# The end of a two-layer block's MLP: folds on another engine, the last eighth of the down projection in token order, and a parked residual in other buffers

## The chip, the cores and the metric

The kernel runs on one core of one Trainium2 chip. The metric is device time in microseconds (us); the number for a kernel is the median of several runs. Before the change it is 1811.55 us (three runs, 1811.48 to 1811.81).

## The reference, cut to what matters

Two layers act on a residual stream h of 512 tokens by 1024 features, in float32. Each layer has a mixer (attention and retention), then an MLP, then a gated per-layer embedding (PLE). The change lies between the MLP and the PLE gate:

```python
u = rms_norm(h, norm_mlp_pre[i])
ff = jnp.square(jax.nn.relu(u @ w_mlp_up[i])) @ w_mlp_down[i]      # 1024 -> 4096 -> 1024
h = h + rms_norm(ff, norm_mlp_post[i])
gate = jax.nn.sigmoid(rms_norm(h) @ w_ple_gate[i])                   # 1024 -> 1024
h = h + gate * rms_norm(p[i] @ w_ple_proj[i], norm_ple[i])
```

The norm of the MLP's output needs a sum over all 1024 features of a token, and so does the norm that feeds the gate. So the gate's product for a token can begin only after its whole row of the down projection is there.

## The kernel before, in words

**Precision.** Every matrix product is made of three: each operand is split into a rounded high part and a low part (the rest), and high x high, high x low and low x high are added in PSUM (the list `HL`). So each 128-row piece of a contraction takes three matmuls of 512 columns. For a weight tile of 128 x 1024 the high part is an ACT copy (L273) and the low part a DVE subtraction (L297). `chunk(key)` (L285) returns a split weight tile and, on the way, issues the fetches (`load`, L246, from SP) and the splits (`prefetch`, L266) of the items up to three ahead. The split tiles share a ring of five buffers (`wp`, L202), so a tile's split waits until the tile five items earlier has been read for the last time.

**Order of the work.** The order of TensorE's (PE) instructions is that of the program. The other engines' instructions are ordered by the framework's scheduler before the run; `soon` (L371) gives what it wraps a priority that is 300 places higher. `step` (L321) counts groups of matmuls; after a given number of them (`AGE_DN` = 6 for the down projection) it lets the oldest entry of `pending` issue its PE work. `settle` (L385) issues the entries of given token tiles at once. In `pre_norm` (L389) the second half of a norm, the four plus four PE transposes of a token tile with their evacuations on ACT (high part, L412) and DVE (low part, L413), is such an entry. Each group of four transposes needs one of the two PSUM banks named `tp`.

**The MLP.** The 4096 hidden features come in 32 groups of 128 (`up_job`). Seven eighths of the down projection (`UNITS` = 7) are done by a seven-product block scheme: each eighth has seven products `P1` to `P7` of combinations of hidden blocks with combinations of weight blocks (`product`, L839), and each product is added into an SBUF sum of 128 x 1024 (`prod`, L806, evacuated by DVE at L856). After the last unit the seven sums are combined by seven additions, the folds (`FOLD`, L807; issued at L907 on DVE): four behind `P6`, and one each behind `P3`, `P4` and `P2`. What is left in `P2`, `P3`, `P4`, `P5` is the output of seven eighths, for four token tiles of 128 and two halves of 512 features.

**The last eighth.** Its four hidden groups (`ff`, 28 to 31) are split into high and low parts directly: ACT takes the ReLU (L884) and the rounded square (L887), DVE the exact square (L888) and the low part (L889). The weights are four tiles: two per half of the output features. `row_job` (L328) runs the first half for the four token tiles together, weight tile by weight tile (four PSUM banks `acc`), and then the second half token tile by token tile. Each (token tile, half) has 12 matmuls in two steps of six. `evac_dn` (L919) adds or subtracts the sum in SBUF (DVE, L923), takes the sum of squares (ACT, L347), and multiplies by the norm's gain (L925: POOL for the first half, DVE for the second). After the second half it makes the row's factor (POOL, L355 and L357), updates the residual (DVE, L916), and starts the next norm (`pre_norm`: ACT L347, POOL L355 and L357, DVE L399).

**The parked residual.** Before the MLP, h is written to DRAM (`hm`). At L908 it is fetched back into four 128 x 1024 buffers of the group `A` (eight buffers, also used by the products' operands and the `ff` tiles). The group `X` has two buffers; it holds the sums of weight blocks that POOL makes for the block scheme (L258, L261) and, in the next layer, the two rope tables (`cs_tile`, L655).

**The gate.** `row_job` at L954 runs the PLE gate, first half of its features for token tiles 0 and 1, then 2 and 3. Each pair begins with `settle`.

Of the kernel before, what the change touches and what calls it, by code (L numbers as in the profile page):

```python
# [12 lines left out]
ALU = mybir.AluOpType  # L13
# [4 lines left out]
P = 128  # L18
S = 512
D = 1024  # L20
NL = 2
NT = S // P
# [19 lines left out]
ALL, PAIRS, ONES = ((0, 1, 2, 3),), ((0, 1), (2, 3)), ((0,), (1,), (2,), (3,))  # L42
# [3 lines left out]
AGE_DN = 6  # L46
# [9 lines left out]
UNITS = 7  # L56


def _dn(e, hf, k):
    return 8 * (e // 2) + 4 * hf + 2 * (e % 2) + k  # L60
# [138 lines left out]
def block(ctx: ExitStack, tc: tile.TileContext, x, pT, w, dl, gains, cs, lc, rel, eye, out):  # L199
    nc = tc.nc  # L200
# [11 lines left out]
    def blk(tag, shape, dt=F32, name="blk"):  # L212
        return big.tile(shape, dt, name=name, tag=tag, bufs=NAMES[tag])

    def t2(name="t2"):
        return tmp.tile([P, S], F32, name=name, tag="t")
# [4 lines left out]
    def bank(tag):  # L221
        b = banks[tag].pop(0)
        banks[tag].append(b)
        return b
# [41 lines left out]
    def prefetch(to_raw, to_split):  # L266
        while loaded[1] < min(to_split, len(ITEMS)):
            m = loaded[1]
            key, src = ITEMS[m]
            load(max([n for n in src if n != "chain"]) + 1)  # L270
            r = raw[src[0]] if len(src) == 1 else total(key, src)
            t = wp.tile([P, 2, 1024], F32R, name="wt", tag="wt", bufs=5)
            nc.scalar.activation(t[:, 0, :], r, AF.Copy)  # L273
            n = src[-1]
            pool = len(src) == 1 and (PLAN[n][1] in POOL_LOW and n % POOL_MOD or PLAN[n][1:] in POOL_MORE)
            for sl in HALVES if pool else (slice(0, D),):
                low(nc.gpsimd if pool else nc.vector, t[:, 1, sl], r[:, sl], t[:, 0, sl])
            wt[m] = t
            loaded[1] += 1
            for n in src:  # L280
                if LAST.get(n) == m:
                    raw.pop(n, None)
        load(to_raw)

    def chunk(*key):  # L285
        m = ITEM[key]
        n = max(x for _, src in ITEMS[max(0, m - 3):m + 4] for x in src if x != "chain")
        prefetch(n + 3, m + 4)
        return wt[m]
# [26 lines left out]
    def row_mm(ps, ch, j, lhs, k, t, first, last):  # L316
        for n, (a, b) in enumerate(HL):
            nc.tensor.matmul(ps, lhsT=lhs(a, k, t), rhs=ch[:, b, j * S:(j + 1) * S],  # L318
                             start=first and n == 0, stop=last and n == 2)

    def step(age=None):  # L321
        clock[0] += 1
        age = AGE if age is None else age
        if pending and clock[0] - pending[0][0] >= age:
            soon(pending.pop(0)[1])()
        tick()

    def row_job(keys, lhs, evac, groups=ALL, age=None):  # L328
        n = len(keys)
        chs = {}  # L330
        for grp in groups:
            if lhs is u_lhs:
                settle(grp)
            pss = [bank(ROW_BANKS[n]) for n in range(len(grp))]
            for c in range(len(keys)):
                if grp is groups[0]:
                    chs[c] = chunk(*keys[c])
                for t, ps in zip(grp, pss):
                    for j in range(2):
                        row_mm(ps, chs[c], j, lhs, 2 * c + j, t, c == 0 and j == 0, c == n - 1 and j == 1)  # L340
                    if c == n - 1:
                        evac(t, ps)
                    step(age)
# [27 lines left out]
    def soon(f, offset=None):  # L371
        offset = PRIO if offset is None else offset

        def g(*a):
            if not offset:
                return f(*a)
            with tc.high_priority(offset=offset):
                return f(*a)
        return g
# [5 lines left out]
    def settle(ts):  # L385
        while any(t in unready for t in ts):
            soon(pending.pop(0)[1])()
# [59 lines left out]
    def tick():  # L447
        if side["gen"] is None:
            return
        side["owed"] += side["rate"]  # L450
        while side["owed"] >= 1.0:
            side["owed"] -= 1.0
            if soon(lambda: next(side["gen"], None), BG)() is None:
                side["gen"] = None
                return
# [179 lines left out]
    def one_layer(i, h):  # L635
# [102 lines left out]
        h = [blk("V", [P, D], name="h") for _ in range(NT)]  # L738
# [3 lines left out]
        for c in range(8):  # L742
            th = ths[c] if c in ths else b_gate(c)
            ps = bank("acc")
# [37 lines left out]
        for hf in range(2):  # L782
            hsl = slice(hf * S, (hf + 1) * S)
            ch = chunk(i, "pp", hf)
            for t in range(NT):
                ps = bank(PP_BANKS[4 * hf + t])
# [19 lines left out]
        prod = {x: blk("V", [P, 2, S], name=f"sum{x}") for x in PROD}  # L806
# [4 lines left out]
        def dn_bank():  # L811
            b = dn_banks.pop(0)
            dn_banks.append(b)
            return b
# [7 lines left out]
        def operands(f1, f2):  # L822
            a11, a21, a12, a22 = f1[:, :, :256], f1[:, :, 256:], f2[:, :, :256], f2[:, :, 256:]
            ops = {}
            x, y, z, v = (t2(n).rearrange("p (s n) -> p s n", s=2) for n in ("sx", "sy", "sz", "sv"))
            operand(ops, "P1", a11)
            nc.vector.tensor_tensor(x, a22, a21, op=ALU.subtract)
            operand(ops, "P5", x)
            nc.vector.tensor_tensor(z, a11, a21, op=ALU.subtract)
            operand(ops, "P7", z)  # L830
            nc.vector.scalar_tensor_tensor(y, x, -1.0, a11, op0=ALU.mult, op1=ALU.subtract)
            operand(ops, "P6", y)
            nc.vector.scalar_tensor_tensor(v, y, -1.0, a12, op0=ALU.mult, op1=ALU.subtract)
            operand(ops, "P3", v)
            operand(ops, "P4", a22)
            operand(ops, "P2", a12)
            return ops
# [21 lines left out]
        for j in range(2):  # L859
            settle(PAIRS[j])  # L860
            for c in range(EARLY):
                if not j:
                    early.append(bank(EARLY_BANKS[c]))
                t = chunk(i, "up", c)
# [8 lines left out]
        half_f = []  # L873

        def up_job(c):
            if c < EARLY:
                ps = early[c]
            else:
                ps = bank("s")
                t_job((i, "up", c), ps)  # L880
            if 2 <= c < 6:
                ple_norm(c - 2)
            r = t2("relu")
            nc.scalar.activation(r, ps, AF.Relu)  # L884
            if c >= 4 * UNITS:
                b = blk("A", [P, 2, S], F32R, name="ff")
                nc.scalar.activation(b[:, 0, :], r, AF.Square)  # L887
                nc.vector.tensor_tensor(r, r, r, op=ALU.mult)  # L888
                nc.vector.tensor_tensor(b[:, 1, :], r, b[:, 0, :].bitcast(F32), op=ALU.subtract)  # L889
                half_f.append(b)  # L890
                return
            if c % 2 == 0:
                half_f.append(blk("P", [P, 2, S], name="f"))
            nc.scalar.activation(half_f[-1][:, c % 2, :], r, AF.Square)
# [3 lines left out]
        for e in range(UNITS):  # L898
            ops = operands(*half_f)
            half_f = []  # L900
            for n, xs in enumerate((("P1", "P5"), ("P7", "P6"), ("P3", "P4"), ("P2",))):
                up_job(4 * e + 4 + n)
                for name in xs:
                    product(e, name, ops[name])
                    if e == UNITS - 1:
                        for to, of in FOLD.get(name, ()):
                            nc.vector.tensor_tensor(prod[to], prod[to], prod[of], op=ALU.add)  # L907
        for t in range(NT):  # L908
            h[t] = blk("A", [P, D], name="hr")
            nc.sync.dma_start(h[t], hm[t])  # L910

        acc = [[prod[x][:, t % 2, :] for x in (("P2", "P3"), ("P4", "P5"))[t // 2]] for t in range(NT)]
# [6 lines left out]
        def evac_dn(hf):  # L919
            @soon  # L920
            def f(t, ps):
                a = acc[t][hf]
                nc.vector.tensor_tensor(a, ps, a, op=ALU.subtract if hf else ALU.add)  # L923
                ssq[t][hf] = sumsq(a, t2("junk"), None if hf else 1e-6)
                (nc.vector if hf else nc.gpsimd).tensor_tensor(a, a, g_mpost[:, HALVES[hf]], op=ALU.mult)  # L925
                if hf:
                    pre_norm(h[t], t, None, upd_mlp(t, rstd_of(*ssq[t])))
            return f

        for hf in range(2):  # L930
            row_job([(i, "dn", _dn(UNITS, hf, k)) for k in range(2)],
                    lambda a, k, t: half_f[k][:, a, t * P:(t + 1) * P], evac_dn(hf), ONES if hf else ALL, AGE_DN)

        if not last:
            g_next = gain_row(5 * (i + 1))
# [19 lines left out]
        if last:  # L955
            t, f = NT - 1, evac_pg(1)
            for j in range(CUTS):
                cut = slice(j * S // CUTS, (j + 1) * S // CUTS)
                n = cut.stop - cut.start
                ps = bank("acc")  # L960
# [9 lines left out]
    h = [blk("V", [P, D], name="h") for _ in range(NT)]  # L970
# [25 lines left out]
    for i in range(NL):  # L996
        h = one_layer(i, h)
# [29 lines left out]
```

## Time and profile before

| what | value |
|---|---|
| median of 3 runs | 1811.55 us |
| the profiled execution, its own time | 1810.16 us |
| its span (first to last instruction) | 1808.4 us |
| PE busy | 1773.1 us, 98% of the span |
| VectorE (DVE) busy | 1215.8 us, 67% |
| ScalarE (ACT) busy | 822.1 us, 45% |
| GpSimd (POOL) busy | 496.1 us, 27% |
| mean granted clock of TensorE | 0.994 |

How to read it: times in rows are us from the start of the span, unless ns is said. A timeline row gives start, length, engine, line, operation, output<-inputs, shapes and how many instructions it merges; in brackets stands the idle time of the engine before it and what ended it. Matmuls are pipelined: in a merged row the length divided by the count is their spacing, while a single one is listed as about 389 ns long. Some matmul records are missing, so counts can be a little low.

### The profile page before, as it was taken

The numbers are of one execution on the slowest core, as the hardware profiler recorded it, in microseconds if no ns is written. First come the engines' busy times: TensorE is split into PE (matmuls) and PEld (weight loads), VectorE is DVE, ScalarE is ACT, GpSimd is POOL, SyncE is SP. The second block draws the span as 40 slices with busy tenths as digits, with TensorE's granted clock in tenths as the row PEclk, the third lists the DMA queues.
The fourth block names the chain that finished last, engine by engine and source line by source line (L and its number), as shares of the span: only waits on it lengthen the run. The fifth ranks groups of instructions, "written<-read, shape, count | busy, mean of one in ns | idle before, by whom it ended". The sixth has DMA issues, their size and how long they took to land.

```text
span 1808.4 us, 22117 instructions
## 1 busy us (share of the span) xinstructions
PE 1773.1 (98%) x8185; PEld 1466.0 (81%) x8185; DVE 1215.8 (67%) x1839; ACT 822.1 (45%) x1291; POOL 496.1 (27%) x370
## 2 busy tenths in 40 slices
PE   8999999999999999998999999999999999999989
PEld 6888788888888888887888887888888888888867
DVE  6676768743557787788556767677444677777873
ACT  4355454422456454544343555443234574544442
POOL 2312144301165222222023222442012642222130
PEclk9999999999999999999999999999999999999989
DMA  5554464432343222334246545554232422333231
GB/s 214 200 182 157 156 209 148 144 140 93 111 146 117 94 94 97 113 122 158 94 140 212 166 149 171 180 164 169 98 112 97 137 94 99 111 107 104 94 140 47
DMA packets 79165, 243.10 MB, mean 134 GB/s; under 512 B 10961, under 2 KB 19537, under 8 KB 79058
## 3 DMA queue, kind: packets, MB, share of 16 engines
q1 hardware_dynamic: 79058, 241.70, 39.9%
q8 instruction: 64, 1.05, 0.2%
q14 instruction: 43, 0.35, 0.1%
HBM read 208.10 MB, written 33.55 MB: 134 GB/s over the span
## 4 chain that ended last, share of the span: by engine, by line
PE 87%; DVE 5%; POOL 3%; ACT 2%; issue 1%; DMA 1%; SPq 0%; ACTq 0%; POOLq 0%
PE acc L308 27%; PE s L308 17%; PE acc L318 17%; PE acc L845 10%; PE tp L845 5%; PE tp L608 2%; POOL wt L297 2%; PE tp L540 2%; PE tp L503 2%; PE acc L867 1%; ACT wt L273 1%; PE tp L409 1%; PE s L521 1%; DVE wt L297 1%; PE s L522 1%
## 5 line engine op out<-in xcount | busy, mean ns | idle before, releaser
L308 PE MATMUL acc<-uT,wt 128*128 128x512 f32 x1920 | 472.9, 393 | 0.0
L308 PEld LDWEIGHTS acc<-uT,wt 128*128 128x128 f32 x1920 | 356.5, 188 | 71.5
L273 ACT ACTIVATE wt<-raw 128x1024 fp32r<-128x1024 f32 x278 | 293.4, 1056 | 225.6 <-PE acc L308 114.5
L297 DVE TENSOR_TENSOR wt<-raw,wt 128x1024 fp32r<-128x1024 f32 x211 | 291.6, 1389 | 131.5 <-ACT wt L273 130.6
L318 PE MATMUL acc<-wt,uT 128*128 128x512 f32 x1320 | 324.2, 399 | 4.0 <-DVE uT L413 1.7
L308 PE MATMUL s<-uT,wt 128*128 128x512 f32 x1392 | 324.7, 389 | 0.0
L308 PEld LDWEIGHTS s<-uT,wt 128*128 128x128 f32 x1392 | 261.3, 188 | 54.0
L297 POOL TENSOR_TENSOR wt<-raw,wt 128x512 fp32r<-128x512 f32 x134 | 184.9, 1401 | 409.8 <-ACT wt L273 370.6
L318 PEld LDWEIGHTS acc<-wt,uT 128*128 128x128 f32 x1320 | 248.1, 191 | 55.8 <-DVE uT L413 2.9
L845 PE MATMUL acc<-wt,op 128*128 128x512 f32 x792 | 188.0, 389 | 0.0
L845 PEld LDWEIGHTS acc<-wt,op 128*128 128x128 f32 x792 | 148.7, 188 | 30.8
L261 POOL TENSOR_TENSOR wsum<-raw 128x1024 f32<-128x1024 f32 x28 | 74.7, 2667 | 210.1 <-DMA raw<-in_w_dram 210.1
L258 POOL TENSOR_TENSOR wsum<-wsum,raw 128x1024 f32<-128x1024 f32 x28 | 71.1, 2539 | 167.6 <-DVE wt L297 167.6
L856 DVE TENSOR_TENSOR sumP<-acc,sumP 128x512 f32<-128x512 f32 x112 | 75.5, 686 | 61.6 <-PE acc L845 61.1
L884 ACT ACTIVATE relu<-s 128x512 f32<-128x512 f32 x60 | 35.5, 592 | 175.7 <-PE s L308 175.7
L297 DVE TENSOR_TENSOR wt<-wsum,wt 128x1024 fp32r<-128x1024 f32 x56 | 83.9, 1498 | 15.4 <-ACT wt L273 15.4
L845 PE MATMUL tp<-wt,op 128*128 128x512 f32 x384 | 92.3, 389 | 0.0
L308 PE MATMUL acc<-retT,wt 128*128 128x512 f32 x384 | 89.3, 389 | 0.0
L845 PEld LDWEIGHTS tp<-wt,op 128*128 128x128 f32 x384 | 72.1, 188 | 14.9
L308 PEld LDWEIGHTS acc<-retT,wt 128*128 128x128 f32 x384 | 72.1, 188 | 14.9
L300 ACT ACTIVATE rt<-rz 128x512 fp32r<-128x512 f32 x64 | 40.3, 632 | 90.0 <-DVE rz L590 89.5
L526 ACT ACTIVATE z<-z,nm 128x512 f32<-128x512 f32 x64 | 46.2, 722 | 56.6 <-DVE nm L525 56.3
(166 smaller groups left out, 2232.3 us busy)
## 6 DMA issues: line engine op xcount, KB each, us to landing
raw<-in_w_dram SPq DMA_DIRECT2D x292, 512.0 KB, 3.3
kk<-stk SPq DMA_DIRECT2D x128, 128.0 KB, 4.1
stq<-rr SPq DMA_DIRECT2D x16, 512.0 KB, 3.4
qs<-stq SPq DMA_DIRECT2D x128, 64.0 KB, 2.8
stk<-rr SPq DMA_DIRECT2D x16, 512.0 KB, 3.0
stv<-vr SPq DMA_DIRECT2D x16, 512.0 KB, 4.8
vh<-stv SPq DMA_DIRECT2D x16, 512.0 KB, 4.3
gain<-in_gains_dram SPq DMA_DIRECT2D x9, 512.0 KB, 3.8
```

The source lines that it names most:

```text
L258: nc.gpsimd.tensor_tensor(r, r, b, op=ALU.add)
L261: nc.gpsimd.tensor_tensor(r, raw[src[0]], raw[src[1]], op=ALU.add)
L273: nc.scalar.activation(t[:, 0, :], r, AF.Copy)
L297: eng.tensor_tensor(dst, src, hi.bitcast(F32), op=ALU.subtract)
L300: nc.scalar.activation(dst[:, 0], src, AF.Copy, scale=scale)
L308: nc.tensor.matmul(ps, lhsT=t[:, a, (off + k) * P:(off + k + 1) * P], rhs=r, start=k == 0 and n == 0, stop=k == kts - 1 and n == 2)
L318: nc.tensor.matmul(ps, lhsT=lhs(a, k, t), rhs=ch[:, b, j * S:(j + 1) * S], start=first and n == 0, stop=last and n == 2)
L503: nc.tensor.matmul(o, lhsT=v, rhs=pt[k][:, hl, :], start=k == 0 and hl == 0, stop=k == 3 and hl == 1)
L526: nc.scalar.activation(z, z, AF.Exp, bias=nm, scale=-1.0, accum_out=den)
L540: nc.tensor.transpose(ps[:, t * P:(t + 1) * P], zs[t][:, k * P:(k + 1) * P], ident)
L845: nc.tensor.matmul(ps, lhsT=op[:, a, k, j * P:(j + 1) * P], rhs=t[:, b, k * S:(k + 1) * S], start=k == 0 and n == 0, stop=k == 1 and n == 2)
L856: nc.vector.tensor_tensor(a, ps, a, op=ALU.add)
```

## The change

The seven folds are issued on POOL instead of DVE. The parked residual of token tiles 0 and 1 is fetched into group `X` and only that of tiles 2 and 3 into `A`. The last eighth calls `chunk` for all its four weight tiles first and then runs token tile by token tile: for each, both halves of the features, each from four pieces of the contraction, with PSUM banks taken from the six that the products use (`dn_bank`: the four `acc` and the two `tp`). `evac_dn` and the step count are as before.

```diff
--- before.py
+++ after.py
@@ -904,9 +904,9 @@
                     product(e, name, ops[name])
                     if e == UNITS - 1:
                         for to, of in FOLD.get(name, ()):
-                            nc.vector.tensor_tensor(prod[to], prod[to], prod[of], op=ALU.add)
+                            nc.gpsimd.tensor_tensor(prod[to], prod[to], prod[of], op=ALU.add)
         for t in range(NT):
-            h[t] = blk("A", [P, D], name="hr")
+            h[t] = blk("X" if t < 2 else "A", [P, D], name="hr")
             nc.sync.dma_start(h[t], hm[t])
 
         acc = [[prod[x][:, t % 2, :] for x in (("P2", "P3"), ("P4", "P5"))[t // 2]] for t in range(NT)]
@@ -927,9 +927,16 @@
                     pre_norm(h[t], t, None, upd_mlp(t, rstd_of(*ssq[t])))
             return f
 
-        for hf in range(2):
-            row_job([(i, "dn", _dn(UNITS, hf, k)) for k in range(2)],
-                    lambda a, k, t: half_f[k][:, a, t * P:(t + 1) * P], evac_dn(hf), ONES if hf else ALL, AGE_DN)
+        tail = [chunk(i, "dn", _dn(UNITS, hf, k)) for hf in range(2) for k in range(2)]
+        for t in range(NT):
+            for hf in range(2):
+                ps = dn_bank()
+                for k in range(4):
+                    row_mm(ps, tail[2 * hf + k // 2], k % 2, lambda a, k, t: half_f[k][:, a, t * P:(t + 1) * P], k, t, k == 0, k == 3)
+                    if k == 3:
+                        evac_dn(hf)(t, ps)
+                    if k % 2:
+                        step(AGE_DN)
 
         if not last:
             g_next = gain_row(5 * (i + 1))
```

## Rows read from the trace of the kernel before

**Rows 1.** The page's first part: busy time and share of each engine.

```profile
PE 1773.1 (98%) x8185; PEld 1466.0 (81%) x8185; DVE 1215.8 (67%) x1839; ACT 822.1 (45%) x1291; POOL 496.1 (27%) x370
```

**Rows 2.** Timeline of PE, layer 0, last eighth to the gate's first product.

```profile
828.93 20.56 PE L318 MATMUL acc<-wt,ff 128*128 128x512 f32 x90
849.69 1.09 PE L409 MATMUL tp<-ident,un 128*128 128x128 f32 x8 [0.20 <-DVE un L399]
850.54 1.64 PE L318 MATMUL acc<-wt,ff 128*128 128x512 f32 x6
858.43 1.11 PE L409 MATMUL tp<-ident,un 128*128 128x128 f32 x4 [6.25 <-DVE ss L349]
860.99 1.12 PE L409 MATMUL tp<-ident,un 128*128 128x128 f32 x4 [1.45 <-DVE uT L413]
861.76 8.92 PE L318 MATMUL acc<-wt,uT 128*128 128x512 f32 x30
```

**Rows 3.** Timeline of PE, layer 1, the same two waits.

```profile
1753.56 1.11 PE L409 MATMUL tp<-ident,un 128*128 128x128 f32 x4 [6.25 <-DVE ss L349]
1756.12 1.12 PE L409 MATMUL tp<-ident,un 128*128 128x128 f32 x4 [1.45 <-DVE uT L413]
```

**Rows 4.** Windows of PE: length, busy (x), granted clock, DMA share, GB/s.

```profile
852.18:855.44 3.26, 0.00 (x1) 1.00 0.02 4
855.44:865.69 10.25, 5.81 (x17) 0.50 0.30 103
...
1747.31:1749.74 2.43, 0.00 (x0) 1.00 0.01 3
1749.74:1759.98 10.24, 4.97 (x15) 0.50 0.15 52
```

**Rows 5.** Timeline, layer 0: evacuations of the first transposed tile, ACT then DVE.

```profile
853.52 0.57 ACT L412 ACTIVATE uT<-tp 128x512 fp32r<-128x512 f32 x1
...
857.69 0.68 DVE L413 TENSOR_TENSOR uT<-tp,uT 128x512 fp32r<-128x512 f32 x1
...
860.26 0.68 DVE L413 TENSOR_TENSOR uT<-tp,uT 128x512 fp32r<-128x512 f32 x1
```

**Rows 6.** The folds: busy per engine from 811.9, the line L907, DVE's timeline.

```profile
811.90:832.60 20.70, 20.70 (x93) 17.12 (x92) 20.13 (x24) 7.32 (x9) 0.00 (x0) 1.00 0.48 175
...
L907 DVE TENSOR_TENSOR sumP<-sumP,sumP x14: 1214/1217/1228, 811.9 to 1725.8; 128x1024 f32<-128x1024 f32 x14
...
810.75 1.22 DVE L297 TENSOR_TENSOR wt<-raw,wt 128x1024 fp32r<-128x1024 f32 x1
...
824.99 2.35 DVE L297 TENSOR_TENSOR wt<-raw,wt 128x1024 fp32r<-128x1024 f32 x2
...
831.85 0.68 DVE L889 TENSOR_TENSOR ff<-relu,ff 128x512 fp32r<-128x512 f32 x1
```

**Rows 7.** Timeline where POOL and DVE meet in layer 0: POOL, then DVE.

```profile
718.15 2.40 POOL L258 TENSOR_TENSOR wsum<-wsum,raw 128x1024 f32<-128x1024 f32 x1 [12.61 <-DVE wt L297]
...
718.00 0.68 DVE L856 TENSOR_TENSOR sumP<-tp,sumP 128x512 f32<-128x512 f32 x1
718.60 4.17 DVE L297 TENSOR_TENSOR wt<-raw,wt 128x1024 fp32r<-128x1024 f32 x2
```

**Rows 8.** Timeline, three POOL operations in a row beside DVE; last row: DVE undisturbed.

```profile
505.39 4.69 POOL L297 TENSOR_TENSOR wt<-raw,wt 128x512 fp32r<-128x512 f32 x3
...
505.45 3.48 DVE L402 SCALAR_TENSOR_TENSOR un<-h,rstd,gain 128x512 f32<-128x512 f32 x2 [2.94 <-POOL rstd L357]
...
896.65 1.41 DVE L402 SCALAR_TENSOR_TENSOR un<-hr,rstd,gain 128x512 f32<-128x512 f32 x2 [1.69 <-POOL rstd L357]
```

**Rows 9.** Residual fetches (SP), their first use (DVE), first use of the rope tables.

```profile
826.65 2.79 SPq L910 DMA_DIRECT2D hr<-hm  x4
...
846.05 1.41 DVE L916 SCALAR_TENSOR_TENSOR hr<-sumP,rstd,hr 128x512 f32<-128x512 f32 x2 [0.71 <-DMA raw<-in_w_dram]
...
L472 DVE TENSOR_TENSOR ra<-acc,cst x4: 680/687/692, 940.0 to 957.0; 128x512 f32<-128x512 f32 x4
```

## The prediction
> **What bounds the kernel now.** I read the page's shares first: PE is busy 98% of the span [rows 1], so only what moves PE's end counts, and PE's remaining idle time is where to look. PE's timeline at the end of layer 0's last eighth [rows 2] shows it. Its 96 matmuls begin at 828.93 and go at 0.228 us each (20.56 / 90), 1.37 us per step of six. The transposes of token tile 0 come 15 steps in and wait 0.20 us for their norm. The eighth ends at 850.54 + 1.64 = 852.18; then PE waits 6.25 us before the transposes of tile 1 and 1.45 us between their two groups: 7.9 us idle. Layer 1 repeats the two large waits to the hundredth [rows 3].
>
> There is a second price. The granted clock is 1.00 up to 3.26 us into this idle time (2.43 us in layer 1), then 0.50, the lower of the two levels, for 10.24 us [rows 4]. PE is busy 5.81 us of that in layer 0 and 4.97 us in layer 1, so half is lost: 2.9 and 2.5 us. So this place costs 10.8 us in layer 0 and 10.4 us in layer 1, **21.2 us** in all.
>
> Why the wait? The row's releaser is a small DVE operation, but that is only the semaphore's last count. The tile-1 transposes need a `tp` bank that still holds tile 0's. ACT reads the first group at 853.52; DVE reads it only at 857.69 and the second at 860.26 [rows 5], and PE's two groups start right behind. DVE is late because the second half of the eighth hands it a whole token tile every two steps (2.7 us): two residual updates (1.41 as a pair, [rows 9]) and, of the same kind as the 0.68 us operations of [rows 5], one subtraction, one gain, two evacuations of the transposes, and two norm scalings: over 4.5 us.
>
> **The change part by part.**
>
> Token order. Each tile now takes four steps (5.5 us) and both its halves end together, so DVE gets about 5 us of work per 5.5 us, and the norm of tile 0 starts after step 4, not step 10. Today's tile-0 norm takes 7.2 us from the end of step 10 (842.5) to 849.69 [rows 2]; its transposes are still issued six counts later, after step 9, 5 steps or 6.8 us behind the evacuation: 0.4 us of wait. Tile 1's come after step 13, inside the eighth. So the two waits go, if DVE keeps up: minus 21.2, plus 0.4 per layer, plus about 0.6 per layer for the gate's first products waiting for tile 1's evacuation (between 0, if DVE is free, and the 1.45 us of [rows 2]).
>
> Folds. A fold costs DVE 1.22 us [rows 6], 1.14 from start to start (824.99 has two in 2.35). The nearest POOL row, an addition of the same shape, is 2.40 us [rows 7]. By busy time alone DVE gains 7 x 1.14 = 8.0 us of the 20.13 it is busy in the 20.7 us after the first fold [rows 6]. But DVE and POOL exclude each other here: a pair of L297, 2.35 us when POOL is idle, takes 4.17 us when it starts 0.45 us into a 2.40 us POOL addition: it waited for that to end [rows 6, 7]. DVE operations that read one operand from PSUM do not wait: L856 keeps its 0.68 us across the POOL operation's start [rows 7]. With several POOL operations in a row the two take turns: L402 pairs go from 1.41 to 3.48 us [rows 8]. The Trainium skill ("SBUF — State Buffer", section "Who interferes with whom") calls it an exclusive lock held for a whole instruction, taken by GpSimd operations that read SBUF and DVE operations with two SBUF inputs; the trace agrees. That page does not say who is next; if POOL kept the pair through the four folds behind `P6`, 9.6 us by the 2.40 us row, DVE would be blocked all that time at once; the turns of [rows 8] speak against it.
>
> So from 811.9 (the first L297 after `P6` ends, [rows 6]) I add up the lock. POOL needs 7 x 2.40 = 16.8 us. Until the last `ff` low part DVE has five L297 (1.14) and four of L888 and L889 (0.60) with both operands in SBUF: 8.1 us. With turns and no gap: 811.9 + 24.9 = 836.8, plus two evacuations of `P2` at 0.6 which the seventh fold itself awaits: **838.0**. If the seventh fold comes behind that low part, it is 835.6. Before, it was done at 832.5 [rows 6].
>
> Now who waits? Before, the pieces k = 2 and 3 of the contraction came after four steps, at 834.4; in the new order k = 3 comes with matmul 10, at 828.93 + 9 x 0.228 = 831.0. So PE waits **4.6 to 7.0 us** there. The clock would fall about 2.8 us into that wait (between the 2.43 and 3.26 of [rows 4]), at 833.8, until 844.1; PE, resuming at 835.6 to 838.0, runs 8.5 to 6.1 us at half speed and loses 4.3 to 3.0. Wait and clock together: 8.9 to 10.0 us per layer, oddly insensitive to the length of the wait.
>
> Residual in `X`. Today's fetches land some 6 us after 826.65, and the first use is at 846.05 [rows 9]; the first use moves to about 838, still covered. Nothing gained; at most 1 us if a fetch blocks SP's queue of weight fetches, which runs two items or more ahead. The next layer's rope tables must now wait until tiles 0 and 1 are done in the gate, near 896.65 + 1.41 [rows 8]; they are first used at 940.0 [rows 9], so nothing. The folds pass no other POOL work: POOL is idle there (0.00, [rows 6]).
>
> Four `chunk` calls first, six banks. The ring has five buffers and four are held by the eighth to its last steps, so the second gate tile is split only after step 13 instead of after step 4. From there to its use are 3 steps, the transposes of tile 1 and 2 gate steps, 7.6 us; its split needs two operations of 1.2 us (ACT's estimated from DVE's L297). Nothing, up to 2 us per tile if DVE is behind. The `tp` banks, now shared: tile 1's last subtraction (0.68) ends before tile 0's transposes: 0 to 0.5 us.
>
> **The sum.** Per layer: removed 10.8 or 10.4, added 8.9 to 10.0 plus 0.4 plus 0.6. Net -0.9 to +0.2 in layer 0 and -0.5 to +0.6 in layer 1; both layers -1.4 to +0.8. The profiled execution took 1810.16 us (span 1808.4), 1.4 below the median; added to it, 1810.2 to 1812.4. I say **1811.0 us**: a stall changes places. With 2 us more or less per layer for DVE's order, 1806.5 to 1815.
>
> **The rivals.**
>
> 1. Faster: the low part of `ff` 31 comes early in DVE's order, ahead of the last weights' L297, and only one or two folds delay it. For it: the 8 us that DVE is relieved of. Against: the lock sum. Without a lock it would be done at 831.4 (832.5 less a fold): wait 0.4; with two L297 behind it, 835.6 - 2.3 = 833.3: wait 2.3, short enough to keep the clock. With the 1.0 of the later waits and up to 1.5 for a late weight tile, the loss is 1.4 to 4.8 per layer in place of 10.6: 1811.55 - 2 x (5.8 to 9.2) = 1793 to 1800, likeliest 1797. Chance 0.25.
>
> 2. Slower: the weight ring. The stall stays as forecast, and behind it the gate's second to fourth weight tiles, freed one step apart at the eighth's end, queue on DVE behind the norms of tiles 2 and 3. Each L297 (1.14) has an in-order queue with some 5 us of norm work before it; it decides once the first is over 5 us late (7.6 less 2.4). Then PE waits 2 to 4 us per layer: 1815 to 1819. For it: DVE is the late engine there today [rows 5]. Against: token order spreads its work. Chance 0.19.
>
> 3. The change does not do what it says, as something else holds tile 1's transposes: time unchanged, inside the forecast's range; chance 0.01, the forecast 0.55.
>
> **How the numbers follow.** About 0.2% (3.6 us) is what a measurement of this kernel can tell from no change. Below 1807.9: rival 1 with 0.25 and the forecast's lower edge, 0.09. Above 1815.2: rival 2 with 0.18 and the forecast's upper edge, 0.07. The rest, 0.41, is no change. The range reaches into both rivals, 1796 to 1816.5, leaving out about 0.08 at either end.
>
> **What would show it.** Right: no idle time before L409 behind the eighth; a PE wait of 4 to 8 us at the tenth matmul of the eighth, released by DVE's L889; L297 and L889 beside the folds at 2 to 3.5 us; folds 2.4 to 3.6 us each; a window of clock 0.50 some 3 us into that wait. Wrong: L889 done before 833 and no half clock, or the 6.25 us wait still there.

## The result, and the profile after

The changed kernel takes 1822.62 us (median of 4 runs, 1821.28 to 1825.62); the kernel before took 1811.68 us (median of 4). The ratio is 1.0063, with a 95% interval of 1.0045 to 1.008: it is **slower** by 11 us. The forecast of 1811.0 us and its range, 1796 to 1816.5, missed it; its sign was that of the second rival.

The profiled execution took 1823.24 us (span 1821.5), 13.1 us of span more than before. This is PE's timeline of the changed kernel at the same place in layer 0, and the rows of layer 1 where it waits; it answers to [rows 2, 3].

```profile
829.58 2.65 PE L318 MATMUL acc<-wt,ff 128*128 128x512 f32 x11
838.54 5.15 PE L318 MATMUL acc<-wt,ff 128*128 128x512 f32 x13 [6.30 <-DVE ff L889]
...
851.27 0.66 PE L409 MATMUL tp<-ident,un 128*128 128x128 f32 x4 [0.78 <-DVE un L399]
852.33 0.66 PE L409 MATMUL tp<-ident,un 128*128 128x128 f32 x4 [0.40 <-DVE sumP L923]
...
860.20 0.66 PE L409 MATMUL tp<-ident,un 128*128 128x128 f32 x4 [1.28 <-DVE ss L349]
860.61 4.37 PE L318 MATMUL acc<-wt,ff 128*128 128x512 f32 x18
865.82 1.62 PE L318 MATMUL acc<-wt,uT 128*128 128x512 f32 x6 [0.84 <-DVE sumP L923]
870.02 4.56 PE L318 MATMUL acc<-wt,uT 128*128 128x512 f32 x12 [2.58 <-DVE sumP L923]
...
880.75 1.03 PE L409 MATMUL tp<-ident,un 128*128 128x128 f32 x8
...
1739.80 5.08 PE L318 MATMUL acc<-wt,ff 128*128 128x512 f32 x13 [6.30 <-DVE ff L889]
...
1771.20 4.55 PE L318 MATMUL acc<-wt,uT 128*128 128x512 f32 x12 [2.58 <-DVE sumP L923]
```

The old waits of 6.25 and 1.45 us are gone. In their place stand a wait of 6.30 us for the low part of the last hidden group (L889), three smaller ones at the transposes (2.46 us together), and two at the gate's first products for L923, the subtraction of the eighth's last token tile (0.84 and 2.58 us).

To compare versions I use one stretch, from the eighth's first matmul to the transposes of tile 3. In the changed kernel it is 880.75 - 829.58 = 51.17 us in layer 0 and 51.09 in layer 1. These are its last rows in the kernel before, layer 0 and 1:

```profile
874.15 1.03 PE L409 MATMUL tp<-ident,un 128*128 128x128 f32 x8
...
1768.86 1.03 PE L409 MATMUL tp<-ident,un 128*128 128x128 f32 x8
```

There it is 874.15 - 828.93 = 45.22 and 1768.86 - 1724.06 = 44.80 us. So the two stretches hold 5.95 + 6.29 = 12.2 of the 13.1 us; the rest is spread over the execution (0.65 us of it are there when the first stretch begins).

The windows of PE in the changed kernel (length, busy, granted clock, DMA share, GB/s) show that the clock falls twice per layer:

```profile
832.24:835.83 3.59, 0.00 (x0) 1.00 0.84 302
835.83:842.66 6.83, 4.12 (x10) 0.50 0.58 225
867.44:869.97 2.53, 0.00 (x0) 1.00 0.00 0
869.97:873.38 3.41, 3.36 (x8) 0.50 0.68 199
```

It falls 3.59 us into the wait for L889, for 6.83 us, and at the end of the 2.58 us wait, for 3.41 us. Half of the busy time in these is lost: 2.06 and 1.68 us.

Why L889 is late stands in DVE's timeline of the changed kernel, and then POOL's:

```profile
819.89 2.29 DVE L888 TENSOR_TENSOR relu<-relu 128x512 f32<-128x512 f32 x1
...
822.71 2.29 DVE L889 TENSOR_TENSOR ff<-relu,ff 128x512 fp32r<-128x512 f32 x1
824.91 0.68 DVE L856 TENSOR_TENSOR sumP<-tp,sumP 128x512 f32<-128x512 f32 x1
825.52 6.16 DVE L297 TENSOR_TENSOR wt<-raw,wt 128x1024 fp32r<-128x1024 f32 x2
...
833.93 0.68 DVE L888 TENSOR_TENSOR relu<-relu 128x512 f32<-128x512 f32 x1
834.53 3.35 DVE L297 TENSOR_TENSOR wt<-raw,wt 128x1024 fp32r<-128x1024 f32 x1
837.81 0.68 DVE L889 TENSOR_TENSOR ff<-relu,ff 128x512 fp32r<-128x512 f32 x1
...
811.57 10.06 POOL L907 TENSOR_TENSOR sumP<-sumP,sumP 128x1024 f32<-128x1024 f32 x3 [8.10 <-DVE sumP L856]
824.40 6.20 POOL L907 TENSOR_TENSOR sumP<-sumP,sumP 128x1024 f32<-128x1024 f32 x2
834.09 2.72 POOL L907 TENSOR_TENSOR sumP<-sumP,sumP 128x1024 f32<-128x1024 f32 x1 [3.49 <-DVE sumP L856]
```

A DVE operation with both operands in SBUF that meets a fold waits for it: 2.29 us for one of 0.68, 6.16 for a pair of 2.35 [rows 6]. The folds wait too: three take 10.06 us, not 7.2. Evacuations from PSUM (L856) keep their 0.68. The last fold begins at 834.09, between L888 and L889, and holds the L297 that stands between these; L889 ends at 838.49.

And this is DVE at the norms of tiles 0 and 1 and at the start of the gate, changed kernel, and then POOL:

```profile
849.72 1.89 DVE L399 TENSOR_SCALAR un<-hr,rstd 128x512 f32<-128x512 f32 x2 [1.03 <-POOL rstd L357]
...
857.58 1.97 DVE L399 TENSOR_SCALAR un<-hr,rstd 128x512 f32<-128x512 f32 x2 [0.43 <-POOL rstd L357]
...
866.19 0.87 DVE L399 TENSOR_SCALAR un<-hr,rstd 128x512 f32<-128x512 f32 x2
866.98 0.15 DVE L349 TENSOR_SCALAR ss<-ss 128x1 f32<-128x1 f32 x1
867.04 2.23 DVE L297 TENSOR_TENSOR wt<-raw,wt 128x1024 fp32r<-128x1024 f32 x1
869.20 0.68 DVE L923 TENSOR_TENSOR sumP<-acc,sumP 128x512 f32<-128x512 f32 x1
...
849.66 1.28 POOL L925 TENSOR_TENSOR sumP<-sumP,gain 128x512 f32<-128x512 f32 x1
...
857.98 1.28 POOL L925 TENSOR_TENSOR sumP<-sumP,gain 128x512 f32<-128x512 f32 x1 [0.44 <-ACT junk L347]
...
866.81 1.39 POOL L925 TENSOR_TENSOR sumP<-sumP,gain 128x512 f32<-128x512 f32 x1 [0.74 <-ACT junk L347]
```

The subtraction for tile 3 stands behind the norm of tile 2 and a low part of the gate's weights in DVE's order. Until it has run, the bank is not free, and the gate's second product has been given that bank.

The same rows show that POOL holds DVE up at a second place, where no fold is left. The gain of the first half (L925) is on POOL, as it was before, but in token order that of the next tile falls beside a norm. The pair of L399 at the gate takes 0.87 us; those of tiles 0 and 1, each beside an L925, take 1.89 and 1.97, although L399 reads only one tensor from SBUF. The L297 ahead of the last subtraction takes 2.23 us instead of 1.22, beside a third L925. So about 1.0 us each of the waits of 1.28 and 2.58 us, and all of the 0.78, is this (an estimate from these lengths). In the kernel before none of the 16 L399 takes over 0.49 us. No run here moves this gain to DVE.

### The profile page after: what moved, and what is told of

Read it like the earlier page. It is cut to its first block, busy times and chain, and to the rows that moved or that the text cites. A ratio compares the mean times of both kernels' runs of the same rounds, so it can differ in the third digit from the quotient of the medians.

```text
span 1821.5 us, 22108 instructions
## 1 busy us (share of the span) xinstructions
PE 1777.3 (98%) x8185; PEld 1466.0 (80%) x8185; DVE 1229.4 (67%) x1825; ACT 822.4 (45%) x1291; POOL 538.3 (30%) x384
## 4 chain that ended last, share of the span: by engine, by line
PE 85%; DVE 7%; POOL 3%; ACT 2%; issue 2%; DMA 1%; SPq 0%; ACTq 0%; POOLq 0%; DVEq 0%
PE acc L308 28%; PE s L308 17%; PE acc L318 16%; PE acc L845 9%; PE tp L845 4%; PE tp L608 2%; POOL wt L297 2%; PE tp L540 2%; PE tp L503 1%; DVE wt L297 1%; PE acc L867 1%; PE s L521 1%; PE s L522 1%; PE tp L409 1%; PE s L586 1%
## 5 line engine op out<-in xcount | busy, mean ns | idle before, releaser
L297 DVE TENSOR_TENSOR wt<-raw,wt 128x1024 fp32r<-128x1024 f32 x211 | 307.4, 1464 | 124.8 <-ACT wt L273 123.9
L297 POOL TENSOR_TENSOR wt<-raw,wt 128x512 fp32r<-128x512 f32 x134 | 185.1, 1403 | 409.6 <-ACT wt L273 371.2
L856 DVE TENSOR_TENSOR sumP<-acc,sumP 128x512 f32<-128x512 f32 x112 | 75.7, 686 | 61.8 <-PE acc L845 61.2
L297 DVE TENSOR_TENSOR wt<-wsum,wt 128x1024 fp32r<-128x1024 f32 x56 | 88.2, 1575 | 15.3 <-ACT wt L273 15.3
L748 POOL TENSOR_TENSOR fT<-m,fT 128x512 f32<-128x512 f32 x16 | 22.8, 1424 | 167.8 <-DVE m L747 167.8
```

The source lines that it names most:

```text
L297: eng.tensor_tensor(dst, src, hi.bitcast(F32), op=ALU.subtract)
L856: nc.vector.tensor_tensor(a, ps, a, op=ALU.add)
```

## The experiments

My theory after reading this trace was of two separate costs, and left the gain on POOL out. POOL's folds delay DVE's two-operand work (the lock), and the eighth's six-bank rotation leaves the gate's first pair with the banks of the last token tile (the bank takeover). The rivals were that the token order by itself makes DVE late, and that the gate would be held at the same place by its weights anyway. In the first four runs the kernel before had a median of 1810.84 us, in the second four 1811.53 us. "The stretch" below is that of layer 0.

**Folds back on DVE**, in the changed kernel:

```diff
-                            nc.gpsimd.tensor_tensor(prod[to], prod[to], prod[of], op=ALU.add)
+                            nc.vector.tensor_tensor(prod[to], prod[to], prod[of], op=ALU.add)
```

> The changed kernel with its seven folds back on DVE; all else as changed. Theory (POOL's folds and DVE's operations with two SBUF operands shut each other out, so the last low part of ff comes late): PE's 6.30 us wait for L889 falls to at most 1.6 us and the half clock behind it goes, some 8 us per layer: 1804 to 1810. Rival (the new token order by itself makes DVE late): the wait for L889 stays above 4 us and the time stays at 1818 or more.

Measured: 1808.62 us, ratio 0.9987 (0.9977 to 0.9997). PE's timeline:

```profile
828.09 2.65 PE L318 MATMUL acc<-wt,ff 128*128 128x512 f32 x11
831.75 3.24 PE L318 MATMUL acc<-wt,ff 128*128 128x512 f32 x13 [1.00 <-DVE ff L889]
...
861.30 4.38 PE L318 MATMUL acc<-wt,uT 128*128 128x512 f32 x12 [2.58 <-DVE sumP L923]
...
871.86 1.03 PE L409 MATMUL tp<-ident,un 128*128 128x128 f32 x8
```

The wait for L889 falls from 6.30 to 1.00 us, the half clock behind it goes (1.00 from 832 to 842), and nothing else moves: the 2.58 us at the gate are unchanged. The stretch is 43.77 us, 7.40 less. Beside the folds on POOL, the seven L297 of 810 to 840 had a median of 2.82 us; here it is 1.22. The theory holds; at L889 the token order is not late by itself.

**The folds alone on POOL**, in the kernel before (the reverse of that edit).

> The kernel before with the folds alone moved to POOL. Theory (lock): L889 ends near 838 here too; the old order wants it only at about 835, so PE waits about 3 us there, on top of the old waits of 6.25 and 1.45 us: 1816 to 1822. Rival (the folds cost nothing by themselves, only the new order feels them): 1811 to 1813.

Measured: 1816.07 us, ratio 1.003 (1.0019 to 1.0041). PE's timeline:

```profile
828.31 7.27 PE L318 MATMUL acc<-wt,ff 128*128 128x512 f32 x29
837.33 14.16 PE L318 MATMUL acc<-wt,ff 128*128 128x512 f32 x61 [1.76 <-DVE ff L889]
...
860.00 1.12 PE L409 MATMUL tp<-ident,un 128*128 128x128 f32 x4 [6.24 <-DVE ss L349]
```

L889 is just as late, 837.3, but the old order wants it only at 835.58: a wait of 1.76 us, shorter than the 3 us expected, on top of the old 6.24. So the folds cost something in either order, and most in the new one, which asks for the last hidden group 4.6 us sooner (2.65 in place of 7.27 us after its first matmul).

**Four of the folds on POOL** (those behind `P6`), three on DVE, in the changed kernel:

```diff
-                            nc.gpsimd.tensor_tensor(prod[to], prod[to], prod[of], op=ALU.add)
+                            (nc.gpsimd if name == "P6" else nc.vector).tensor_tensor(prod[to], prod[to], prod[of], op=ALU.add)
```

> The changed kernel with only the four folds behind P6 on POOL and the last three on DVE. Theory (lock: each fold on POOL delays DVE's two-operand work by up to its 2.4 us): the wait for L889 lies between the 1.0 us of none and the 6.3 us of seven, at 2 to 4 us, and the clock stays up if it is below 2.4: 1810 to 1817. Rival (only the last fold, which falls among the last operations of ff, hurts): wait about 1.0, 1807 to 1810.

Measured: 1815.15 us, ratio 1.0019 (1.0009 to 1.0028). PE's timeline, then its windows:

```profile
836.01 4.83 PE L318 MATMUL acc<-wt,ff 128*128 128x512 f32 x13 [2.63 <-DVE ff L889]
...
836.01:836.92 0.91, 0.91 (x4) 1.00 1.01 405
836.92:840.33 3.41, 3.41 (x10) 0.50 0.91 362
```

The wait grows with the number of folds on POOL: 1.00, 2.63, 6.30 us for none, four and seven. The last three folds are on DVE here, so it is not only the fold beside L889 that delays it, but those beside what stands ahead of it in DVE's queue. The clock fell here too, 0.91 us after the wait was over.

**Other banks for the gate**, in the changed kernel: the rotation is moved on by two.

```diff
+        bank("acc"), bank("acc")
         for hf in range(2):
             row_job([(i, "pg", 4 * hf + c) for c in range(4)], u_lhs, evac_pg(hf), PG_GRP[2 * i + hf], AGE_PG[hf])
```

> The changed kernel, with the rotation of the acc banks moved on by two before the gate, so that its first two products no longer take the banks of the eighth's last token tile. Theory (bank takeover): the waits of 0.84 and 2.58 us for L923 and the second stretch at half clock go, some 5 us per layer: 1811 to 1815. Rival (the gate's weight tiles, split late because of the ring, or DVE's order, hold the same place): the wait passes to L297 or L413 and the time stays at 1819 to 1823.

Measured: 1815.37 us, ratio 1.0027 (1.0017 to 1.0037). PE's timeline at the gate:

```profile
864.66 3.11 PE L318 MATMUL acc<-wt,uT 128*128 128x512 f32 x13
869.19 1.43 PE L318 MATMUL acc<-wt,uT 128*128 128x512 f32 x5 [1.42 <-DVE wt L297]
...
876.82 1.04 PE L409 MATMUL tp<-ident,un 128*128 128x128 f32 x8
```

Both waits for L923 go, and the second low stretch of the clock with them: the stretch is 47.22 us, 3.95 less. The time lies just above what was expected, because 1.42 us came back as a wait for the gate's second weight tile (L297): the rival holds in this part. That L297 takes 2.26 us, beside POOL's L925, so about 1.0 of the 1.42 us is POOL's gain again (an estimate as above).

**Both edits together.**

> The changed kernel with both: folds on DVE and the gate's banks moved on by two. Theory (the two costs are separate and add): 1794 to 1801, clearly below the kernel before. Rival (one stall hides the other, or DVE, loaded with the folds again, makes the norms late): 1804 to 1812.

Measured: 1801.26 us, ratio 0.995 (0.9936 to 0.9965): faster than the kernel before, and 21 us below the changed kernel's 1822.62 of the earlier session. The stretch is 869.16 - 829.03 = 40.13 us:

```profile
832.68 3.24 PE L318 MATMUL acc<-wt,ff 128*128 128x512 f32 x13 [1.00 <-DVE ff L889]
...
843.50 0.66 PE L409 MATMUL tp<-ident,un 128*128 128x128 f32 x4 [0.78 <-DVE un L399]
844.56 0.66 PE L409 MATMUL tp<-ident,un 128*128 128x128 f32 x4 [0.40 <-DVE sumP L923]
...
852.42 0.66 PE L409 MATMUL tp<-ident,un 128*128 128x128 f32 x4 [1.27 <-DVE ss L349]
...
861.56 1.42 PE L318 MATMUL acc<-wt,uT 128*128 128x512 f32 x5 [1.42 <-DVE wt L297]
...
829.03:869.16 40.13, 35.26 (x163) 1.00 0.31 115
```

The last row is the window of that stretch, up to the transposes of tile 3 at 869.16: clock 1.00 throughout. The gains add: 7.40 + 3.95 = 11.35 us expected from the two runs above, 11.04 measured. So the two costs are separate.

**The residual of tiles 0 and 1 in group `A` again**, in that version (`blk("A", ...)` for all four).

> The version with folds on DVE and the gate's banks moved on, and the residual of tiles 0 and 1 fetched into group A again. Theory (the fetch is covered either way): the same as that version within 2 us, 1799 to 1803, no PE wait for a fetch. Rival (the early fetch into X is what lets the new order run): tile 0's norm waits for its residual, 2 us or more per layer: 1805 or more.

Measured: 1802.47 us, ratio 0.9948 (0.9933 to 0.9963); the stretch is 873.37 - 833.19 = 40.18 us and no wait is new. The move of the residual is worth nothing that these runs can tell.

**Only the four `acc` banks in the eighth**, folds on DVE, and no extra rotation:

```diff
-                ps = dn_bank()
+                ps = bank("acc")
```

> The changed kernel with folds on DVE, and the last eighth taking only the four acc banks in their own rotation, which also gives the gate the banks of tile 2 instead of tile 3. Theory (both bank conflicts are of the six-bank rotation's making): as the version with moved banks, and the 0.40 us wait for L923 before the transposes goes too: 1798 to 1801. Rival (a new wait for L923 inside the eighth, as a tile's banks come round after two tiles): 1802 or more.

Measured: 1800.65 us, ratio 0.9935 (0.9918 to 0.9951). The 0.40 us wait for L923 and the 1.42 us for L297 go, but the stretch, 869.78 - 829.63 = 40.15 us, is the same. The window behind the transposes of tile 1 says where it went:

```profile
853.18:856.59 3.41, 3.41 (x11) 0.50 0.00 0
```

The clock fell there. So this version and that with both edits are equal within their intervals, and both beat the kernel before.

**Transposes one step later**, in the last version: `step(AGE_DN + 1)` in the eighth.

> As the one with acc banks only, and the transposes of a norm issued one step later in the last eighth (7 counts instead of 6). Theory (PE's 0.78 us before tile 0's transposes is only that the norm is not ready): that wait and most of the 1.28 us behind it go, 1 to 2 us per layer: 1796 to 1799. Rival (the gate's first weights, 1.42 us late behind L297, take the place): no gain, 1799 to 1802.

Measured: 1811.39 us, ratio 0.9999 (0.9987 to 1.0011). Neither was right. PE's timeline:

```profile
844.10 1.03 PE L409 MATMUL tp<-ident,un 128*128 128x128 f32 x8
...
858.47 0.73 PE L318 MATMUL acc<-wt,uT 128*128 128x512 f32 x2 [0.73 <-ACT uT L412]
863.41 3.92 PE L318 MATMUL acc<-wt,uT 128*128 128x512 f32 x10 [4.21 <-DVE uT L413]
```

The 0.78 us before tile 0's transposes are gone as expected, but tile 1's, a step later too, miss a place in DVE's order: their low part (L413) falls behind two of the gate's L297 and the norm of tile 2, and the gate waits 4.21 us for it. By the medians that step costs some 11 us (1811.39 against 1800.65).

## Why the prediction was wrong, point by point

**The old bound.** Right. In token order the waits of 6.25 and 1.45 us are gone, and once the two new costs are taken out the stretch falls from 45.22 to 40.13 us.

**The folds.** Right in kind and size. The turns of the lock put L889's end at 838.0; it ended at 838.49. That it came so close is partly luck: I had counted five L297 and no gap, but six run from 811.9 on, as DVE's order now has one ahead of L889, and POOL is idle for 3.49 us before the last fold. The wait also began at the twelfth matmul, 832.2, and not at the tenth, 831.0: of a piece's three matmuls only the last reads the low part. PE's wait was to be 4.6 to 7.0 us and was 6.30. Wait and clock were to cost 8.9 to 10.0 us per layer; they cost 6.30 + 2.06 = 8.4, as the clock stayed low for 6.83 us, not 10.24. The first rival, DVE relieved and unhindered, fell with the run that put the folds back.

**The token order's own waits.** Under-sized. I put 0.4 us at tile 0's transposes and 0.6 at the gate for tile 1's evacuation. Measured at the transposes: 0.78, 0.40 and 1.28 us, 2.46 per layer. I had priced POOL against DVE for the folds alone; most of this time is the same exclusion by POOL's gain (L925), which the token order brings beside the norms. The 0.40 is the `tp` bank of tile 1, inside its bound of 0 to 0.5. The gate waited for no evacuation of tile 1.

**Four `chunk` calls first, six banks: this step failed.** I had looked at the `tp` banks and not at the four `acc` ones. By the program the gate draws the same two `acc` banks in both kernels, as the eighth's eight draws from four banks had left that rotation where it was; what the change altered is who used them last. Before, that was the second half of tiles 0 and 1, subtracted by 843.9 and 848.1, long before the gate; now the six-bank rotation comes round to them for the eighth's last tile. For banks the step had at most 0.5 us; what was measured is 0.84 + 2.58 us of wait and 1.68 us of half clock, 5.1 us per layer, or 10.2 us of a miss of 11.6. Moving the banks gave 3.95 of it back. The other part of this step, the late weight tiles, was the second rival's mechanism: it is there at most in part (1.42 us once the banks are moved, inside the bound of 2 us, and about 1.0 of that is POOL's gain), and it did not decide. That rival had the sign right and the reason wrong.

**The sum, redone.** Per layer 8.4 + 2.5 + 5.1 = 16.0 us added in place of 10.8 in layer 0 gives +5.2; measured +5.95. The remaining 0.8 us lie in PE's busy time, and I have not assigned them.

**The residual.** Right: covered in either group (1802.47 against 1801.26, within their intervals).

## What to carry to other kernels

Work moved from DVE to POOL is not a gift: where the two exclude each other, price it as the sum of both engines' such operations, in turns, up to the first DVE result that another engine waits for. Do the same for what already was on POOL, as a new order can bring it beside DVE's work. When the order of matmuls changes, write down for each PSUM bank who uses it last and who takes it next, over the border to the next stage and in every rotation; the next stage can take the same banks as ever and still wait, because their last user is now a later one. And where DVE's order is fixed beforehand, a wait that is removed can be less important than the operation which happens to stand before the next one that PE needs.

## What the runs showed of the hardware

POOL's L925 held up L399, a DVE operation with one tensor in SBUF: of a pair of 0.87 us it made 1.89 and 1.97. The low clock's stretches were 3.41, 6.83 and 10.24 us long, not one length. It fell after waits as short as 2.63 and 2.58 us, once 0.91 us after PE was busy again; a wait of 1.42 us (both edits) was not followed by one, while in the version with four banks, whose waits at tile 1's transposes are 0.28 and 1.41 us, a stretch of 3.41 us at half clock began right behind. No run here isolates what decides it.
